# RMSNorm and matmul on one core: one 3 MB store cut by partitions into 22 DMAs, 16 of them issued by GpSimd

## The chip, the cores and the metric

The kernel runs on one core of a Trainium2 chip. The core has five engines that run their own instruction streams: TensorE (PE) for matrix products, VectorE (DVE), ScalarE (ACT), GpSimd (POOL) and SyncE (SP). Data moves between the main memory and the core's on-chip memory by DMA: an instruction on one of the engines' queues (SP, ACT or POOL) starts a transfer, and 16 DMA engines carry it out. The metric is the device time of one execution in microseconds, median of several runs. The time before is 208.85 us (208.76 to 209.47 in 3 runs).

## The reference

```python
rms = np.sqrt(np.mean(x ** 2, axis=-1, keepdims=True) + eps)
x_norm = x / rms * gamma
return np.matmul(x_norm, weight).astype(np.float32)
```

x is 16 x 1024 x 512, the weight is 512 x 768, all float32. Flattened, there are 16,384 rows of x: 33.6 MB in, 50.3 MB of results out, and a weight of 1.6 MB.

## The kernel before

**Tiles.** The rows are cut into 128 tiles of 128 rows, one row of a tile on each of the 128 partitions. `rows` (L121) fixes which rows form a tile: inside a group of 16 (or 32) tiles, one partition holds 16 (or 32) neighbouring rows of x, so that a partition's share of eight tiles is one contiguous piece of main memory, 16,384 bytes of x or 24,576 bytes of the result.

**One tile's way.** Loads bring 8 tiles at a time into `xt` (two halves of 16 tiles). POOL casts them to bf16 (`cast`, L188). PE turns them, two bf16 values as one 32-bit word (`transpose_word`, L230), and DVE copies the turned words out (`evac`, L239). Of every 16 tiles the last four go another way: POOL casts them into `xq` (`cast_quad`, L260) and DVE turns them in 32 x 32 blocks (`move`, L271). PE multiplies a tile with the weight (`matmuls`, L300) into one of three accumulators. ACT squares the tile and sums along the row (L196), takes a root (L201), DVE inverts it (L203); the row's factor is applied when the accumulator is read out into `ot`: by ACT for even tiles (L279), by DVE for odd ones (L281). Gamma is folded into the weight at the start.

**The result's way out.** `ot` has three buffers of 8 tiles, taken in turn: tiles 16 to 23 lie in the third one, and tiles 40 to 47 use it next. `store` (L293) issues a DMA on SP's queue when the last tile of a stretch has been written. A stretch has 8 tiles, except at the start (1, 1, 2, 4) and at the end (4, 4, then 4, 2, 2). The kernel has 22 stores, 13 of them of 3,072 KB. Loads from tile 32 on are issued on ACT's queue (L177).

**Order.** Nothing here is scheduled by a tool: the main loop over pairs of tiles (j = 1 to 63; pair j is tiles 2j and 2j + 1) hands each operation to an `Order` object with the cells that it reads and writes. `Order.emit` then writes the streams in just that order, and puts a wait ahead of an operation for each earlier one that its engine doesn't yet know to be done (L93). A DMA counts as a process of its own: each is waited for by itself, on its own semaphore value. So the first operation that overwrites a buffer waits for every DMA that read it. Semaphores are used again for a later DMA once the issuing engine knows the earlier one to be done.

POOL's own stream holds the casts of x, two at a time or more ahead of their use, and no DMA.

## Time and profile before

| | |
|---|---|
| median of 3 runs | 208.85 us |
| the profiled execution's own time | 209.07 us |
| its span, first to last instruction | 207.1 us |
| granted TensorE clock, mean | 0.993 |
| moved by DMA | 85.62 MB, 413 GB/s over the span |
| busy: PE / DVE / ACT / POOL | 194.7 / 149.5 / 144.3 / 60.0 us |

The span of the profiled execution lies 2.0 us under its own time. A line of the profile names an engine, a line of the kernel and the tile written and read (`ot<-ps,rstd` writes `ot` from the accumulators). "SPq", "ACTq" and "POOLq" stand for the queue's own work: issuing a DMA, or waiting on a semaphore. In the list of DMA queues, q1 holds what SP issues and q10 what ACT issues; the "instruction" queues fetch the program itself. Times inside the profile count from the span's start.

### The profile page before, as it was taken

Reading aid. Unit: us, or ns where it says so; the run is one execution under the profiler, and the core shown is the slowest. Engines: PE = TensorE matmul, PEld = TensorE weight load, DVE = VectorE, ACT = ScalarE, POOL = GpSimd, SP = SyncE. Lnnn points to the kernel's source line nnn. Section 1 sums busy time; section 2 is a strip of 40 time slices with the busy share of each in tenths; the row PEclk is TensorE's granted clock in tenths of the full one; section 3 lists DMA queues with packets and bytes.
Section 4 is the critical chain, followed back from the end, with each engine's and each line's share of the span. In section 5 each row is a group of like instructions: output and inputs, shape, how many; then the busy total and the mean of one; then the engine's idle time right before and its main releaser. Section 6 shows DMA issues by size and latency. Waiting matters only on the chain.

```text
span 207.1 us, 2794 instructions
## 1 busy us (share of the span) xinstructions
PE 194.7 (94%) x1236; PEld 72.7 (35%) x717; DVE 149.5 (72%) x255; ACT 144.3 (70%) x343; POOL 60.0 (29%) x34
## 2 busy tenths in 40 slices
PE   7789999999999999999999999999999989999940
PEld 1233434343334334433344333443343324333310
DVE  0446556999579975999579975999569964999530
ACT  4598898777777687777777687676949758683310
POOL 2156752157006340065105170060604224000000
PEclk9999999999999999999999999999999999999997
DMA  6999999999999999999999999999999999999992
GB/s 222 402 434 453 370 419 420 426 461 407 437 429 423 449 419 440 419 434 429 432 449 411 430 434 423 445 423 437 413 424 445 427 440 435 423 437 394 394 412 120
DMA packets 6064, 85.62 MB, mean 413 GB/s; under 512 B 674, under 2 KB 676, under 8 KB 1828
## 3 DMA queue, kind: packets, MB, share of 16 engines
q1 hardware_dynamic: 4320, 60.30, 68.9%
q10 hardware_dynamic: 1732, 25.17, 28.5%
q8 instruction: 7, 0.11, 0.2%
q14 instruction: 5, 0.04, 0.0%
HBM read 35.13 MB, written 50.33 MB: 413 GB/s over the span
## 4 chain that ended last, share of the span: by engine, by line
PE 71%; DMA 17%; DVE 5%; SPq 1%; issue 1%; POOL 1%; ACT 0%; ACTq 0%
PE ps L300 63%; DMA out_dram<-ot 12%; PE ps L230 8%; DMA xt<-in_x_dram 5%; DVE ot L281 2%; DVE xTq L271 2%; DVE xT L239 1%; POOL xb L188 1%; SPq L345 0%; ACT ot L279 0%; SPq L177 0%; DVE rstd L203 0%; SPq L477 0%; ACTq L93 0%; SPq L436 0%
## 5 line engine op out<-in xcount | busy, mean ns | idle before, releaser
L300 PE MATMUL ps<-w_bf,xT 128*128 128x512 bf16 (+1 forms) x800 | 147.9, 326 | 2.1 <-DVE w_bf L281 1.1
L279 ACT ACTIVATE ot<-ps,rstd 128x768 f32<-128x768 f32 x64 | 57.6, 899 | 48.5 <-PE ps L300 37.3
L196 ACT ACTIVATE jk<-xt 128x512 bf16<-128x512 f32 x128 | 78.7, 619 | 1.9 <-DMA xt<-in_x_dram 1.9
L188 POOL CAST xb<-xt 128x2048 bf16<-128x2048 f32 (+3 forms) x21 | 46.4, 2218 | 112.4 <-PE ps L230 69.0
L281 DVE TENSOR_SCALAR ot<-ps,rstd 128x768 f32<-128x768 f32 x64 | 64.8, 1013 | 9.5 <-PE ps L300 8.1
L296 PEld LDWEIGHTS <-xT 128*128 128x128 bf16 x400 | 39.3, 98 | 60.7 <-issue 52.8
L230 PE MATMUL ps<-ident_f,xb 128*128 128x128 f32 x200 | 54.4, 276 | 0.9 <-POOL xb L188 0.9
L239 DVE COPY xT<-ps 128x1024 bf16<-128x1024 bf16 (+1 forms) x53 | 34.5, 654 | 24.2 <-PE ps L230 22.5
L271 DVE STREAM_TRANSPOSE xTq<-xq 32x256 f32<-32x256 f32 x112 | 48.8, 435 | 3.4
L230 PEld LDWEIGHTS ps<-ident_f,xb 128*128 128x128 f32 x200 | 28.3, 143 | 46.6 <-issue 43.3
L300 PE MATMUL ps<-w_bf,xTq 128*128 128x512 bf16 x224 | 42.8, 326 | 0.0
L196 ACT ACTIVATION_READ_ACCUMULATOR jk<-xt 128x1 f32 x128 | 24.4, 190 | 0.0
L296 PEld LDWEIGHTS <-xTq 128*128 128x128 bf16 x112 | 11.0, 98 | 14.5 <-issue 14.5
L260 POOL CAST xq<-xt 128x2048 bf16<-128x2048 f32 x7 | 13.3, 1893 | 0.0
L203 DVE RECIPROCAL rstd<-rms 128x8 f32<-128x8 f32 (+3 forms) x20 | 3.9, 193 | 8.1 <-ACT rms L201 7.9
L201 ACT ACTIVATE rms<-ssq,eps_sb 128x8 f32<-128x8 f32 (+3 forms) x20 | 6.0, 300 | 0.6
L300 PE MATMUL ps<-warm 128*128 128x512 bf16 x10 | 4.5, 588 | 1.4 <-DVE eps_sb L354 1.4
L279 ACT ACTIVATE w_bf<-w_f,g_sb 128x768 bf16<-128x768 f32 x2 | 1.9, 935 | 1.8 <-DMA w_f<-in_weight_dram 1.8
L377 DVE COPY g_sb<-ps 128x4 f32<-128x4 f32 x1 | 0.2, 163 | 3.2 <-PE ps L371 3.2
L341 ACT ACT_TABLE_LOAD x1 | 1.3, 1283 | 1.5 <-SPq L436 1.5
L281 DVE TENSOR_SCALAR w_bf<-w_f,g_sb 128x512 bf16<-128x512 f32 (+2 forms) x3 | 1.4, 482 | 1.2 <-DMA w_f<-in_weight_dram 1.2
L371 PEld LDWEIGHTS ps<-ident_f,g_row 2*128 2x128 f32 x2 | 0.3, 200 | 2.6 <-issue 2.6
(10 smaller groups left out, 2.0 us busy)
## 6 DMA issues: line engine op xcount, KB each, us to landing
out_dram<-ot SPq DMA_DIRECT2D x13, 3072.0 KB, 22.7
xt<-in_x_dram ACTq DMA_DIRECT2D x12, 2048.0 KB, 18.8
xt<-in_x_dram SPq DMA_DIRECT2D x3, 2048.0 KB, 18.2
out_dram<-ot SPq DMA_DIRECT2D x4, 1536.0 KB, 10.9
out_dram<-ot SPq DMA_DIRECT2D x3, 768.0 KB, 6.8
w_f<-in_weight_dram SPq DMA_DIRECT2D x2, 768.0 KB, 5.9
xt<-in_x_dram SPq DMA_DIRECT2D x2, 512.0 KB, 5.4
xt<-in_x_dram SPq DMA_DIRECT2D x1, 1024.0 KB, 9.5
```

The source lines that it names most:

```text
L188: run(POOL, lambda: POOL.tensor_copy(out=xb[s][:, i % 8:i % 8 + n, :], in_=src), of, cells("xb", s, i % 8, n))
L196: run(ACT, lambda: ACT.activation(out=jk[j], in_=src[:, 0, :], func=AF.Square, accum_out=ssq[:, i:i + 1]), of, [("jk", j), ("ssq", i)])
L201: run(ACT, lambda: ACT.activation(out=rms[:, s], in_=ssq[:, s], func=AF.Sqrt, scale=1.0 / D, bias=eps_sb), [("ssq", t) for t in range(i, i ...
L203: run(DVE, lambda: DVE.reciprocal(out=rstd[:, s], in_=rms[:, s]), [("rms", i)], [("rstd", t) for t in range(i, i + n)])
L230: run(PE, lambda: PE.transpose(out=tp[b][:, t, h, :], in_=words[:, lo:lo + P], identity=ident_f), cells("xb", s, j % 4 * 2 + t) + ["ident" ...
L239: run(DVE, lambda: DVE.tensor_copy(out=dst[:, t:t + n, :], in_=src[:, t:t + n, :]), [("tp", b)], cells("xT", j % 4, t, n))
L260: run(POOL, lambda: POOL.tensor_copy(out=xq[s], in_=src), of, [("xq", s)])
L271: run(DVE, lambda: DVE.transpose(out=dst, in_=src), [("xq", s)], [("xTq", s)])
L279: run(ACT, lambda: ACT.mul(out=dst, in_=src, mul=r), reads, writes)
L281: run(DVE, lambda: DVE.tensor_single_scalar(out=dst, in_=src, scalar=r, op=mybir.AluOpType.mult), reads, writes)
L296: run(PE, lambda: PE.ldweights(lhsT), [cell])
L300: run(PE, lambda: PE.add_instruction(mybir.InstMatmult(name=nc.get_next_instruction_name(), engine=mybir.EngineType.PE, ins=[PE.lower_ap(r ...
```

## The change

Only the store of tiles 16 to 23 is changed (`first == XG`, with XG = 16). Before, it is one DMA on SP's queue: 128 partitions, 24,576 bytes of each. After, it is 22 DMAs. Each takes partitions that lie four apart. For p = 0, 1, 2, SP stores partitions p, p + 4, ... p + 24 (seven of them), and the row of partition p + 28 is stored in two halves of 8 x 1,536 bytes, one by SP and one by POOL. For p = 3, 32, 33, 34 and 35, POOL stores the eight partitions p, p + 4, ... p + 28. For all eight p, POOL stores the eight partitions from p + 64 on. SP's six DMAs are issued where the one store was. POOL's sixteen are kept in a list, and put into the order after the next `cast_quad`, that is in the pass j = 15 of the main loop, behind the cast of tiles 44 to 47. A DMA issued by POOL gets a semaphore that no DMA has used before it.

```diff
             if proc is None:
                 free = [k for k, d in enumerate(slots) if known[at].get(("transfer", d), 0)]
-                if free:
+                if free and engine is not nc.gpsimd:
                     slots[free[0]] = n
...
+    later = []
+
+    def spread(dst, src, held):
+
+        def part(engine, p, n, cols=slice(0, O)):
+            at = slice(p, p + 4 * n - 3, 4)
+            move = lambda: order.transfer(engine, lambda: engine.dma_start(out=dst[at, :, cols], in_=src[at, :, cols]), reads=held)
+            later.append(move) if engine is POOL else move()
+
+        for p in (0, 1, 2, 3, 32, 33, 34, 35):
+            if p < 3:
+                part(SP, p, 7)
+                part(SP, p + 28, 1, slice(O // 2, O))
+                part(POOL, p + 28, 1, slice(0, O // 2))
+            else:
+                part(POOL, p, 8)
+            part(POOL, p + 64, 8)
+
     def store(i):
...
             src = ot[s][:, first % OG:first % OG + n, :]
+            if first == XG:
+                spread(rows(out, first, n), src, cells("ot", s, first % OG, n))
+                return
             order.transfer(SP, lambda: SP.dma_start(out=rows(out, first, n), in_=src), reads=cells("ot", s, first % OG, n))
...
             cast_quad((2 * j + 2 + XG - 4) // 4)
+            while later:
+                later.pop(0)()
```

## The prediction

> **What bounds the kernel now.** I read the row of DMA load on the page first, then the busy times by stage, then the waits from the middle on, then the last microseconds, and last the places that the change touches.

> ```profile
> DMA  6999999999999999999999999999999999999992
> ```

> The row holds the mean load of the 16 DMA engines in 40 slices: full from the second slice to the last but one. By stage (columns: stretch, its length, busy us of PE, PEld, DVE, ACT, POOL with counts, granted clock, DMA share, GB/s):

> ```profile
> 50.00:74.00 24.00, 24.00 (x157) 9.08 (x90) 19.62 (x34) 18.05 (x44) 6.90 (x4) 1.00 1.01 432
> 74.00:130.00 56.00, 56.00 (x366) 21.30 (x211) 43.76 (x73) 41.81 (x100) 15.58 (x7) 1.00 1.01 430
> 130.00:168.00 38.00, 37.98 (x247) 14.30 (x142) 32.22 (x56) 26.04 (x63) 10.93 (x4) 1.00 1.00 429
> 168.00:200.00 32.00, 30.28 (x194) 10.76 (x108) 23.49 (x37) 19.63 (x42) 3.73 (x2) 1.00 0.98 418
> 200.00:203.50 3.50, 0.00 (x0) 0.00 (x0) 0.10 (x1) 0.00 (x0) 0.00 (x0) 1.00 0.94 384
> 203.50:205.70 2.20, 0.00 (x0) 0.00 (x0) 0.00 (x0) 0.00 (x0) 0.00 (x0) 0.67 0.06 25
> ```

> Up to 130 PE and the DMA engines are both full. The last line is the odd one: for 2.2 us all five engines are idle and the DMA share is 0.06, one engine in sixteen. The DMA queues in that stretch (packets, MB, share) and the two rows around it:

> ```profile
> q1 hardware_dynamic: 11, 0.06, 6.1%
> ...
> 200.40 0.33 SPq L293 DMA_DIRECT2D out_dram<-ot  x1
> ...
> SPq L477 <- DMA out_dram<-ot: 5.4, 1, 5.4
> ```

> The last store is issued at 200.40. By the trace's packets fifteen engines write their last byte of it by 203.45. One goes on alone with packets of 6,144 bytes, 231 ns apart, until 205.68, and SP waits for it. So 2.2 us of the span belong to a single DMA engine. It is late before the end too. The store issued at 142.43 lands, by the trace's sixteen completions, in three bunches: seven engines at 164.7 to 165.5, eight at 166.3 to 166.6, and one at 167.9. That last one ends a wait of ACT, because tile 104 needs the buffer:

> ```profile
> 142.43 25.50 DMA out_dram<-ot
> ...
> 168.01 0.91 ACT ot L279
> ...
> ACT ot L279 <- DMA out_dram<-ot: 9.5, 4, 3.1
> ```

> ACT has four such waits, 9.5 us in all, all after 128. PE hardly feels them. Its stretches without transposes (36 matmuls) start at 46.69, 70.11, 93.53 and 116.95 in the chain, 23.42 apart for 16 tiles. Three periods after the last the next should start at 187.21, and it starts at 188.32: PE loses 1.1 us to the end.

> The places that the change touches (POOL's rows; one of SP's; ACT's and DVE's first writes into the buffer when it comes round again; a wait instruction; a store's median landing time):

> ```profile
> 48.60 1.89 POOL L260 CAST xq<-xt 128x2048 bf16<-128x2048 f32 x1
> 64.11 3.60 POOL L188 CAST xb<-xt 128x4096 bf16<-128x4096 f32 x1 [13.62 <-PE ps L230]
> ...
> 48.74 0.33 SPq L293 DMA_DIRECT2D out_dram<-ot  x1
> ...
> 71.78 0.90 ACT L279 ACTIVATE ot<-ps,rstd 128x768 f32<-128x768 f32 x1 [0.70 <-PE ps L300]
> 73.58 1.02 DVE L281 TENSOR_SCALAR ot<-ps,rstd 128x768 f32<-128x768 f32 x1
> ...
> L93 ACTq EVENT_SEMAPHORE  x46: 17/17/17, 4.3 to 187.2; - x46
> ...
> out_dram<-ot SPq DMA_DIRECT2D x13, 3072.0 KB, 22.7
> ```

> The store of tiles 16 to 23 is issued at 48.74 and lands at 69.5 by its completions. Tile 40 overwrites the buffer at 71.78.

> **The gain: three rows less on one DMA engine.** A 3,072 KB store is 128 packets of 24,576 bytes, eight an engine, 0.91 us each. SP's three DMAs of seven partitions leave out the eighth of their pattern, partitions 28, 29 and 30. If a row's partition fixes its engine, one engine loses three rows, 2.73 us, and gets back 6 pieces of 1,536 bytes, at 26.6 GB/s 0.35 us: 2.38 us less. Seven others gain 0.35 us each. If that engine is the late one, it ends at 203.3 instead of 205.68, and the others set the end at 203.45 to 203.8. They have idle time to take it from: a share of 0.98 over 168 to 200 is 0.6 us an engine. The end moves by 1.9 to 2.2 us; I take 2.0. The bytes are the same, so no more is to be had than that lag: the fifteen others are full.

> That the engine relieved is the late one no row says. What speaks for it is the shape of the landings, seven, eight and one, the split that the change makes between SP's seven partitions, POOL's eight from p + 64 on, and the one left over. I give it three in four.

> The waits of ACT on the late engine get shorter by its lag (1.3 us in the bunches above). They are worth at most PE's 1.1 us, and as the other DMA engines are full behind them, I count 0.

> **SP.** One issue of 0.33 us becomes six, 2.0 us, and SP then sits until its next store at 59.65: 0. The SP queue has 21.5 rows of this store instead of 128, so the next store finds a shorter queue.

> **POOL.** Sixteen DMAs follow the cast that ends at 50.49; tile 23 has been written by then. The next cast starts at 64.11, and its product is first turned in the pass j = 22, from about 77.2. So POOL has 13.6 us empty and about 9 us more before PE feels it (3.60 us of cast from 73.6). No DMA is issued by POOL in this profile, so its price p is open. The lower end is SP's issue, 0.33 us; the upper is POOL's cast of 128x2048, 1.89 us. I take 1.04, its cast of 128x1024, the middle one of its own rows: 16.6 us, to 67.1, the cast 3.0 us late, cost 0.

> [...]

> **When the pieces land.** Before tile 40 all 22 must have landed. A piece must start (the last store's first fifteen engines need 3.0 us from issue to their last byte, 1.85 of it data), wait for a packet of each other queue (0.91 and 0.61) and move 0.91: 3 us. At p = 1.04 the last lands at 50.5 + 16.6 + 3 = 70.1. At p = 0.33 the engines set the pace: between 50 and 72, q1 and q10 both have work, and their packet counts are alike:

> ```profile
> q1 hardware_dynamic: 258, 5.55, 58.9%
> q10 hardware_dynamic: 268, 3.87, 41.2%
> ```

> So queues take turns by packets. With a third one, eight rows need 8 x (0.91 + 0.91 + 0.61) = 19.4 us, 50.5 to about 71. Both are ahead of 71.78, and SP's own pieces stand behind only the store of 36.2, which lands at 57.4. Loads pay for it: up to 8 packets of 0.91 us, 7.3 us, on the load issued at 53.12. Its first user that can't wait is ACT's square of tile 56 at about 83, 12 us after it landed: 0.

> **Waits.** ACT at tile 40 and DVE at tile 41 wait for 22 DMAs instead of one. A wait lasts 17 ns and the next instruction follows 0.06 us after it begins: 21 x 0.06 = 1.3 us on each. They stand behind the wait for PE, so they start when the product is done. Behind them are queued the read-out and then ACT's squares, DVE's copies for PE. In this stretch a tile takes PE 1.3 us, and tile 43 needs tile 40's accumulator at about 74.3: ACT's read-out, which may start 1.6 us later than 71.78, is just covered, DVE's is some 0.3 us over. PE's 1.1 us of later waiting hide that; without them it costs 0.3 us.

> **Sum.** -2.0 us against the profiled execution's own 209.07 gives 207.1; against the median, which is 0.2 us lower, 208.85 - 2.0 = 206.9. For the likeliest case alone I give 206.3 to 207.7 (another 0.6 us from the waits at one end, 0.8 us of uncovered waits or SP pieces at the other). Less than 0.5% (1.04 us) can't be told from no change in this kernel.

> **Rivals.**
> *The late engine isn't the one relieved.* For it: the profile names no engine. Against it: the seven, eight and one. Then the lag stays, a few engines get 0.35 us more, and the time is 208.8 to 209.2.
> *POOL's eights lie the other way round.* If the engines that carry POOL's rows from p + 64 on are the ones with SP's seven, these get 3 + 8 rows instead of 8, three rows or 2.73 us more, end at 203.45 + 2.73 - 0.6 = 205.6, and no lag is saved: 208.8 to 209.4. Nothing in the profile tells which eight a POOL DMA gets.
> *POOL is too slow, and tile 40 waits.* The wait on the store that now costs ACT nothing at 71.78 becomes the bound. With 1.3 us of waits behind the landing, PE stalls once 50.5 + 16p + 3 is past 72.1, at p = 1.16. PE's 1.1 us cover it up to 1.23, the 2.0 us gained are gone at 1.35, and it is slower by 0.5% from 1.42 on. At 1.89 the last piece lands at 83.7, 11.6 us late: 208.85 + 11.6 - 1.1 - 2.0 = 217.3. For it: POOL's 128x2048 cast, 1.89 us, is past that point, and the margin above my 1.04 is small. Against it: POOL's rows that move little data (0.10 to 0.29 us) come nowhere near 1.4.

> [...]

> **How the numbers follow.** The likeliest case, 206.9, gets 0.52. The wrong engine gets 0.17 and the eights the other way 0.07, both within 0.5%. POOL too slow gets 0.24: 0.01 of it still faster, 0.02 within, 0.21 slower. That makes 0.53, 0.26 and 0.21. The range runs from 206.2, just under the likeliest case, to 211.0, which takes in both middle rivals and POOL up to p = 1.49; the 0.15 beyond it is POOL slower still, up to the 217.3 of its upper row.

> **What would show it.** Right: in the last store's landing all sixteen engines end within half a microsecond, and the stretch of 0.06 DMA share is gone; the chain ends in a DMA of about 3.5 us after its issue; POOL's cast of tiles 48 to 55 starts by 68; ACT's first write after 71 isn't preceded by a wait on a DMA. Wrong: the same lone engine at the end (first rival), several engines late at the end (second), or ACT and PE idle near 72 to 85, with POOL's last DMA issue after 70 (third). The prediction fails most easily by p, of which no row speaks.

## The result and the profile after

The changed kernel takes 232.30 us (median of 4 runs, 231.44 to 233.45) against 208.84 us before in the same comparison: a ratio of 1.112, with a 95% interval of 1.107 to 1.117. The forecast was 206.9 us, and the range ended at 211.0. The profiled execution took 232.22 us, with a span of 230.4 us. Of two kernels in the experiments (one DMA on GpSimd, sixteen partitions each on GpSimd) some executions took clearly longer than the rest; their times are given, but left out of the comparisons.

The first view is again the page's slices of the span: the granted TensorE clock and the load of the DMA engines, in tenths, 5.8 us a slice.

```profile
PEclk9999999999999655559999999999999999999996
DMA  6999999999999974236899999999999999869787
```

Before, the DMA row was full throughout. Now it has a hole from the 15th slice to the 20th, some 81 to 115 us, and the clock drops at its beginning. The table by stage shows the hole (columns: stretch, its length, busy us of PE, PEld, DVE, ACT and POOL with counts, granted clock, DMA share, GB/s):

```profile
68.00:74.00 6.00, 5.73 (x36) 1.88 (x19) 4.73 (x9) 2.12 (x5) 3.73 (x2) 1.00 1.01 383
74.00:84.00 10.00, 0.00 (x0) 0.00 (x0) 0.00 (x0) 0.00 (x0) 0.00 (x0) 0.63 0.96 397
84.00:97.00 13.00, 0.00 (x0) 0.00 (x0) 0.00 (x0) 0.00 (x0) 0.00 (x0) 0.50 0.43 185
97.00:101.00 4.00, 3.04 (x10) 0.68 (x5) 1.74 (x3) 3.99 (x10) 0.00 (x0) 0.50 0.00 0
101.00:105.00 4.00, 3.95 (x18) 1.43 (x11) 0.85 (x2) 1.74 (x5) 0.00 (x0) 0.64 0.74 254
```

From 74 to 97 no engine does anything. The second line still has the DMA engines full. In the third they are idle more than half of the time (0.43), although everything waits for a DMA. That is the line to remember: the transfer that all wait for keeps fewer than half of the DMA engines busy. In the fourth line the DMA engines have nothing at all, because the loads are issued on ACT's queue, and ACT has just come out of its wait: its next load goes out at 101.18.

What they wait for is in the waits (engine, line, releaser: us in total, times, longest) and in the chain of work from 45 to 100 (start, length, what):

```profile
ACT ot L279 <- DMA out_dram<-ot: 26.5, 1, 26.5
DVE ot L281 <- DMA out_dram<-ot: 24.0, 1, 24.0
PE ps L321 <- ACT ot L279: 24.2, 1, 24.2
```

```profile
49.94 7.71 POOL out_dram L294 x15
57.65 39.29 DMA out_dram<-ot
96.94 0.03 ACTq L93
96.97 0.05 issue
97.01 0.91 ACT ot L279
```

ACT's write of tile 40 stands behind the cut store, as it did before. Then the store landed at 69.5, ahead of its need at 71.78. Now its last piece lands at 96.9 and the write starts at 97.01. So 97.01 - 71.78 = 25.2 us are lost in one place. From that write to the end of the span it was 207.1 - 71.78 = 135.3 us before and is 230.4 - 97.01 = 133.4 us now: 1.9 us come back. The sum, +23.3, is the difference of the two spans.

The 1.9 us are nearly the lag of the lone engine at the end. SP's last wait is now

```profile
SPq L500 <- DMA out_dram<-ot: 3.0, 1, 3.0
```

where it was 5.4 us, and the sixteen completions of the last store lie within 0.2 us. That isn't the relief that the change was predicted to give. Every DMA engine had run dry at 101 us, and yet one was late again after that: of the store issued at 133.16, fifteen completions come by 146.6 and the last at 149.5. The lag went later, where the DMA engines had idle time (their share is 0.68 from 200 to 212). In the first experiment below, which was to load all engines alike, the last store's completions also lie within 0.2 us (219.5 to 219.7).

**Why the pieces land so late.** The two rows of POOL's queue on the timeline show that its issues aren't the cause:

```profile
49.88 8.29 POOL L294 DMA_DIRECT2D out_dram<-ot  x16
63.55 3.60 POOL L188 CAST xb<-xt 128x4096 bf16<-128x4096 f32 x1 [5.39 <-PE ps L230]
```

Sixteen issues take 8.3 us, 0.52 us each, and are over at 58.2. POOL then waits 5.4 us for PE before its next cast. The pieces themselves are slow, which their completions show. Each DMA of POOL gives sixteen, as many as there are DMA engines, though none has more than eight rows. For the later DMAs of eight partitions the trace has (us from the span's start):

```
DMA of POOL       eight early ones   eight late ones
p = 3 + 64        60.1 to  63.3      69.3 ... 74.6
p = 32            61.4 to  63.5      73.4 ... 78.6
p = 32 + 64       61.5 to  63.6      77.5 ... 82.8
p = 33            61.7 to  63.8      80.6 ... 85.4
p = 33 + 64       61.9 to  64.0      84.5 ... 88.0
p = 34            62.0 to  64.2      87.3 ... 90.7
p = 34 + 64       62.2 to  64.4      90.0 ... 93.5
p = 35            62.4 to  64.5      92.7 ... 95.5
p = 35 + 64       62.6 to  64.7      93.6 ... 96.9
```

By these times eight engines have nothing to move. The other eight have one row, and each DMA's are a step later than those of the DMA ahead of it. If successive DMAs used different engines, their late completions would run side by side; they run one after the other. So all 13 DMAs lie on one set of eight engines. In each row the first of the late ones is ahead of the second by 0.7 to 2.8 us (80.6 against 83.4 for p = 33): one engine of the set has less to do than the others, as it would if SP's three DMAs of seven partitions used the same set and left one engine out. SP's next store, issued at 59.09, says so too: eight of its completions come at 71.0 to 73.0, one at 80.0 and seven at 83.0 to 86.0. Seven engines therefore carry 3 + 13 = 16 rows of this store, where each had eight; eight engines carry none.

The second thing is the pace. In the last column the steps are 4.0 to 4.2 us at first (74.6 to 82.8) and 2.6 to 2.7 later (82.8 to 93.5), for a row that takes 0.91 us to move. On the first of the late engines the last step is 0.9 us (92.7 to 93.6), the row alone. The DMA queues in two stretches (packets, MB, share of 16 engines), first 72 to 82, with loads (q10), stores of SP (q1) and POOL's pieces (q0), then 84 to 96, where the loads have ended:

```profile
q1 hardware_dynamic: 93, 2.21, 52.8%
q10 hardware_dynamic: 93, 1.39, 36.1%
q0 software_dynamic: 40, 0.49, 11.9%
```

```profile
q1 hardware_dynamic: 73, 1.52, 29.6%
q0 software_dynamic: 76, 0.88, 17.4%
```

In the second, q1 and q0 have the same number of packets, 73 and 76, but not the same bytes: 0.88 MB are 36 rows of 24,576 bytes, and the other 40 of q0's 76 packets are writes of 4 bytes, the signals to the semaphores. The changed kernel has 1,088 packets of 4 bytes where the kernel before has 675. A DMA that brings one row to an engine brings it two packets, the row and the signal, and if each must wait for its own turn, a row costs two rounds of the other queues: 0.91 + 2 x (0.91 + 0.61) = 3.95 us with q1 and q10 busy, 0.91 + 2 x 0.91 = 2.73 with q1 alone. These are the two longer steps measured. The trace's packets show the signal's own turn. Five of them, one after the other (start, length, bytes, queue):

```
85.814  0.912  24,576  q0
86.722  0.912  24,576  q1
87.631  0.009       4  q0
87.636  0.912  24,576  q1
88.545  0.912  24,576  q0
```

The trace doesn't number the DMA engines, so that these five share one is read from their times. It is no accident of one place: of the 20 rows of q0 that end from 84.5 to 92, 19 have a signal of q0 0.88 to 0.93 us behind their end, and of the 23 signals 22 have a row of q0 as long behind them. From 72 to 82, with the loads, the same gaps are 1.51 to 1.58 us, behind 17 of 20 rows and 18 of 20 signals.

One set for all 13 DMAs is what the completions above show. By what rule they are dealt out so, and which engines the set has, no run here shows.

### The profile page after: what moved, and what is told of

Its sections match the earlier page's. It is cut to its first block, busy times and chain, and to the rows that moved or that the text cites. A ratio compares the mean times of both kernels' runs of the same rounds, so it can differ in the third digit from the quotient of the medians.

```text
span 230.4 us, 2811 instructions
## 1 busy us (share of the span) xinstructions
PE 195.7 (85%) x1212; PEld 72.9 (32%) x717; DVE 149.2 (65%) x255; ACT 144.6 (63%) x343; POOL 68.2 (30%) x50
## 3 DMA queue, kind: packets, MB, share of 16 engines
q10 hardware_dynamic: 1732, 25.17, 26.6%
## 4 chain that ended last, share of the span: by engine, by line
PE 69%; DMA 21%; POOL 5%; issue 1%; SPq 1%; DVE 0%; ACT 0%; ACTq 0%
PE ps L321 61%; DMA out_dram<-ot 17%; PE ps L230 8%; DMA xt<-in_x_dram 4%; POOL out_dram L294 3%; POOL xb L188 1%; POOL xq L260 1%; DVE ot L281 0%; ACT ot L279 0%; SPq L366 0%; SPq L177 0%; SPq L500 0%; ACTq L93 0%; SPq L459 0%
## 5 line engine op out<-in xcount | busy, mean ns | idle before, releaser
L321 PE MATMUL ps<-w_bf,xT 128*128 128x256 bf16 (+1 forms) x783 | 146.2, 327 | 26.2 <-ACT ot L279 24.2
L279 ACT ACTIVATE ot<-ps,rstd 128x768 f32<-128x768 f32 x64 | 57.6, 899 | 74.3 <-PE ps L321 46.1
L281 DVE TENSOR_SCALAR ot<-ps,rstd 128x768 f32<-128x768 f32 x64 | 64.8, 1013 | 34.1 <-DMA out_dram<-ot 24.0
L188 POOL CAST xb<-xt 128x2048 bf16<-128x2048 f32 (+3 forms) x21 | 46.4, 2218 | 125.6 <-PE ps L230 107.3
L230 PE MATMUL ps<-ident_f,xb 128*128 128x128 f32 x200 | 54.4, 275 | 0.9 <-POOL xb L188 0.9
L321 PE MATMUL ps<-w_bf,xTq 128*128 128x256 bf16 (+1 forms) x217 | 43.4, 333 | 0.4
L230 PEld LDWEIGHTS ps<-ident_f,xb 128*128 128x128 f32 x200 | 28.3, 142 | 47.3 <-issue 44.0
L317 PEld LDWEIGHTS <-xTq 128*128 128x128 bf16 x112 | 11.2, 100 | 15.3 <-issue 15.3
L260 POOL CAST xq<-xt 128x2048 bf16<-128x2048 f32 x7 | 13.3, 1894 | 0.0
L294 POOL DMA_DIRECT2D out_dram<-ot x16 | 8.3, 526 | 0.0
L279 ACT ACTIVATE w_bf<-w_f,g_sb 128x768 bf16<-128x768 f32 x2 | 1.9, 936 | 1.4 <-DMA w_f<-in_weight_dram 1.4
L281 DVE TENSOR_SCALAR w_bf<-w_f,g_sb 128x512 bf16<-128x512 f32 (+2 forms) x3 | 1.4, 481 | 0.8 <-DMA w_f<-in_weight_dram 0.8
## 6 DMA issues: line engine op xcount, KB each, us to landing
out_dram<-ot SPq DMA_DIRECT2D x12, 3072.0 KB, 16.3
```

Of the source, the lines that this page charges most:

```text
L188: run(POOL, lambda: POOL.tensor_copy(out=xb[s][:, i % 8:i % 8 + n, :], in_=src), of, cells("xb", s, i % 8, n))
L230: run(PE, lambda: PE.transpose(out=tp[b][:, t, h, :], in_=words[:, lo:lo + P], identity=ident_f), cells("xb", s, j % 4 * 2 + t) + ["ident" ...
L260: run(POOL, lambda: POOL.tensor_copy(out=xq[s], in_=src), of, [("xq", s)])
L279: run(ACT, lambda: ACT.mul(out=dst, in_=src, mul=r), reads, writes)
L281: run(DVE, lambda: DVE.tensor_single_scalar(out=dst, in_=src, scalar=r, op=mybir.AluOpType.mult), reads, writes)
L294: move = lambda: order.transfer(engine, lambda: engine.dma_start(out=dst[at, :, cols], in_=src[at, :, cols]), reads=held)
```

## The experiments

All of these kernels compute the whole result. Only the store of tiles 16 to 23 (once, the last two stores) is issued in another way. Each ran beside the kernel before on the same chip, which took 208.8 to 208.95 us.

### Sixteen partitions a piece, all on GpSimd

If uneven engines are the cause, pieces of sixteen partitions, by the author's estimate one row for each engine, must take it away.

```diff
-            at = slice(p, p + 4 * n - 3, 4)
+            at = slice(p, p + 8 * n - 7, 8)
...
-        for p in (0, 1, 2, 3, 32, 33, 34, 35):
-            if p < 3:
...
-            part(POOL, p + 64, 8)
+        for p in range(8):
+            part(POOL, p, 16)
```

> The store of tiles 16 to 23 as eight DMAs of 16 partitions each (p, p+8, ... p+120), all issued by GpSimd at the place where the changed kernel issues its sixteen; nothing of it on SP. Theory A (uneven load: every eight-partition DMA runs on the same eight DMA engines, 13 to 16 rows there instead of 8, and none on the other eight): with 16 partitions a DMA the load is even, the store lands by about 72, ACT waits under 3 us for it at tile 40, and the time is 208 to 210.5 us. Rival B (GpSimd's queue is slow in itself, whatever the engines): more bytes than before go by that queue, the store lands near 96 or later, and the time is 230 us or more. Rival C (the many waits and pieces cost it): eight waits instead of 22, so about a third of the 23 us loss, 214 to 218 us.

Measured: 223.0 us (222.81, 223.00 and 224.13; a fourth execution took 227.12), ratio 1.070, interval 1.065 to 1.074. None of the three ranges expected holds it. The wait at tile 40 ends at 87.5 instead of 97.0 (timeline of this kernel):

```profile
87.48 0.90 ACT L279 ACTIVATE ot<-ps,rstd 128x768 f32<-128x768 f32 x1 [15.95 <-DMA out_dram<-ot]
```

Of the 23.4 us lost, 9.3 are won back and 14.1 stay. If every engine holds eight rows, as that estimate has it, unevenness can't explain the rest. Two things stand out in the trace: between 45 and 100 us 80 of 481 packets of 24,576 bytes took more than 1.2 us, up to 3.2 (before, 1 of 574 did), and again each row has a signal of its own (q0's 256 packets with 3.15 MB are 128 rows and 128 signals). The next runs separate these.

### The same 22 pieces, all on SP

```diff
-            move = lambda: order.transfer(engine, lambda: engine.dma_start(out=dst[at, :, cols], in_=src[at, :, cols]), reads=held)
+            move = lambda: order.transfer(SP, lambda: SP.dma_start(out=dst[at, :, cols], in_=src[at, :, cols]), reads=held)
...
```

> The same 22 pieces at the same places of the order, but all issued on SP's queue; nothing is issued by GpSimd. Theory A (eight-partition DMAs share one set of eight DMA engines, on any queue): these engines still carry 16 rows of the store instead of 8, now in line on SP's queue; tile 40 waits for it for about 10 us or more, the stores after it on SP are late too, and the time is 213 to 230 us. Rival B (GpSimd's queue is slow): no such wait, 208 to 210.5 us, plus at most some us if SP's issues at 1 to 2 us each (20 to 30 us in all) are late.

Measured: 217.16 us (one run), 8.3 us over the kernel before. From the waits and the timeline of this kernel:

```profile
ACT ot L279 <- DMA out_dram<-ot: 11.7, 1, 11.7
```

```profile
82.25 0.90 ACT L279 ACTIVATE ot<-ps,rstd 128x768 f32<-128x768 f32 x1 [11.73 <-DMA out_dram<-ot]
```

The unevenness is there without GpSimd: SP's own eight-partition pieces leave the next store's completions split into eight at 79.8 to 82.1 and eight at 87.2 to 89.4. So a narrow set of engines isn't a peculiarity of GpSimd's queue. SP's pieces go to eight engines too. SP needed 17.0 us to issue the 22 pieces, but the last of them was out by 65.2, 17 us ahead of its landing, so issuing isn't what made it late. What the move to GpSimd's queue adds is 232.3 - 217.2 = 15.1 us. On SP's queue a piece stands behind other pieces of the same queue and takes turns with the loads alone: 0.91 + 2 x 0.61 = 2.13 us a row by the two-turn rule. Measured were 2.1 to 2.2 for the rows that land from 71.5 to 76, and 0.7 to 1.0 for the last five, when the load had ended on these engines.

### Half of the pieces over all engines

```diff
-            part(POOL, p + 64, 8)
+            if p < 4:
+                part(POOL, p + 64, 16)
```

> The changed kernel with one part altered: partitions 64 to 127 go as four DMAs of 16 partitions (64, 68, ... 124 and so on) instead of eight of eight partitions. The same bytes are issued by GpSimd. Theory A: the loaded eight DMA engines get 9 rows from GpSimd instead of 13 (12 with SP's), the other eight get 4. Nine rows at the 3 us or so that each took land near 80, tile 40 waits 7 to 13 us, and the time is 214 to 222 us, about half of the loss. Rival B (GpSimd's queue is slow by bytes): 230 us as with the change.

Measured: 221.0 us (one run), the wait at tile 40 ends at 87.3. Halving the excess rows (four instead of eight) saves 11.3 us of the 23.4, as the uneven-engines theory expects. But pieces of sixteen partitions have a cost of their own, as the first run showed, so this run isn't a clean measure of the dose. The next one is.

### Half of the unevenness, on SP alone

Tiles 16 to 19 as one DMA of all partitions, tiles 20 to 23 as sixteen DMAs of eight partitions, so that eight engines have an excess of four rows instead of eight.

```diff
+            if first == XG:
+                dst, held = rows(out, first, n), cells("ot", s, first % OG, n)
+                order.transfer(SP, lambda: SP.dma_start(out=dst[:, 0:4, :], in_=src[:, 0:4, :]), reads=held)
+                for p in (0, 1, 2, 3, 32, 33, 34, 35):
+                    for at in (slice(p, p + 29, 4), slice(p + 64, p + 93, 4)):
+                        order.transfer(SP, lambda at=at: SP.dma_start(out=dst[at, 4:8, :], in_=src[at, 4:8, :]), reads=held)
+                return
```

> The kernel before, with the store of tiles 16 to 23 on SP as one DMA of four tiles and 128 partitions and sixteen DMAs of eight partitions and four tiles. Theory A (every eight-partition DMA uses the same eight DMA engines): these carry 12 rows instead of 8, the others 4: half the excess of the run with all 22 pieces on SP. That run lost 8.3 us with 16 rows; the excess work is 3.6 us here against 7.3 us, so 2.5 to 6 us are lost, 211.3 to 215 us, and eight of the sixteen completions of the next store come some us after the other eight. Rival (the loss comes from the number of pieces on SP, 17 here and 22 there): 214 to 217 us.

Measured: 212.98 us (one run).

```profile
77.88 0.90 ACT L279 ACTIVATE ot<-ps,rstd 128x768 f32<-128x768 f32 x1 [7.26 <-DMA out_dram<-ot]
```

On SP, an excess of 0, 4 and 8 rows' worth of bytes on eight engines costs 0, 4.0 and 8.3 us, about 1.0 us a row, near the 0.91 us that it takes to move. A cost per piece would have stayed near that of the 22 pieces, since there are still 17 (214 to 217 us was expected for it). The store after it again has eight completions at 76.0 to 81.0 and eight at 84.0 to 85.2. The uneven engines are thus shown as a cause, by the completions and by the size of the loss, though each of the two sizes is from one run.

### The sixteen-partition pieces, on SP

```diff
-            at = slice(p, p + 4 * n - 3, 4)
-            move = lambda: order.transfer(engine, lambda: engine.dma_start(out=dst[at, :, cols], in_=src[at, :, cols]), reads=held)
+            at = slice(p, p + 8 * n - 7, 8)
+            move = lambda: order.transfer(SP, lambda: SP.dma_start(out=dst[at, :, cols], in_=src[at, :, cols]), reads=held)
...
-        for p in (0, 1, 2, 3, 32, 33, 34, 35):
...
+        for p in range(8):
+            part(POOL, p, 16)
```

> The eight DMAs of 16 partitions (p, p+8, ... p+120) of the first experiment, all issued on SP's queue at the same place; GpSimd issues no DMA. The load is even and the queue is the ordinary one. [...] Rival B (only GpSimd's queue made the first experiment slow): packets stay at 0.91 us, the store lands by 72, and the time is 208.3 to 210 us.

Measured: 211.81 us (one run), 2.9 us over the kernel before.

```profile
76.43 0.90 ACT L279 ACTIVATE ot<-ps,rstd 128x768 f32<-128x768 f32 x1 [5.68 <-DMA out_dram<-ot]
```

The pattern of every eighth partition is slow in itself: 50 of 547 packets took over 1.2 us, up to 3.0. The landing is late on two engines most of all: fourteen have completed the last piece by 72.8, the two others at 75.3 and 76.4. Why such packets are slow is not shown. The remaining 223.0 - 211.8 = 11.2 us of the first run come from moving the same pieces to GpSimd's queue.

### The whole store as one DMA on GpSimd

Is a third queue costly by itself, without any cut?

```diff
...
+        later.append(lambda: order.transfer(POOL, lambda: POOL.dma_start(out=dst, in_=src), reads=held))
```

> The whole store of tiles 16 to 23 as one DMA of 128 partitions issued by GpSimd, at the place where the changed kernel issues its sixteen. Two theories after the first three runs. Theory T (turns by packet, and a DMA's semaphore write takes a turn like a packet): a DMA that gives each DMA engine one row has two turns a row, one with eight rows has nine turns for eight. A row then needs 0.91 us of its own and one packet each of SP's and ACT's queue, 2.43 us; eight rows land 19 to 21 us after 51, near 71, tile 40 waits under 2 us, and the time is 208.3 to 210.3 us. Rival B (GpSimd's queue is served slowly whatever it holds, one row in 3 to 4 us as in the changed kernel): 8 rows take 24 to 32 us, landing at 76 to 84, tile 40 waits 4 to 12 us, and the time is 211 to 220 us.

> The one DMA of 128 partitions on GpSimd once more, for its time: the first time it gave 211.3 us once, and 214.9 to 215.4 three times. Theory T (an even DMA on GpSimd costs little): the store lands at 71 to 75 and the time of the undisturbed runs is 211 to 211.6 us, 2.5 us over the kernel before, because one DMA engine falls behind by 3 us on this store. Rival: 214.9 us and more in every run, so that the single 211.3 was the exception.

Measured in both together, nine executions: 210.5, 211.3, 212.6 and 212.9 us, and five of 214.7 to 219.9. By the first four the third queue by itself costs 1.5 to 3.9 us (the second run's ratio is 1.011, interval 1.003 to 1.020, or 2.3 us), and not 15; why the other five took longer is not known. None of the nine lies above 219.9, where the sixteen pieces took 232.3. The time is over the range of the theory of turns (208.3 to 210.3) and mostly inside the rival's (211 to 220), and none of the second run's executions lies in the 211 to 211.6 expected for it, so it doesn't decide between them; the landings do. The profile is of an execution of 215.3 us. The queues from 58 to 70:

```profile
q0 software_dynamic: 97, 2.14, 41.7%
q10 hardware_dynamic: 101, 1.57, 30.6%
q1 hardware_dynamic: 61, 1.43, 28.4%
```

Here q0's packets are whole rows (2.14 MB are 87 of them, so some ten of the 97 packets are signals), and nearly as many as q10's. Its store keeps its share, and fifteen engines land it at 68.6 to 71.3, in time, where the rival had 76 to 84. One engine lands at 74.3, and that one makes tile 40 wait.

### Two DMAs on GpSimd, with rows half as long

If a queue's turn is a packet, halving the packet halves the share of the queue. If turns are by bytes, nothing changes.

```diff
...
+        for t in (slice(0, 4), slice(4, 8)):
+            later.append(lambda t=t: order.transfer(POOL, lambda: POOL.dma_start(out=dst[:, t, :], in_=src[:, t, :]), reads=held))
```

> The same store as two DMAs of 128 partitions and four tiles each, issued by GpSimd at the same place: rows of 12,288 bytes, sixteen packets for a DMA engine instead of eight, the same bytes. Theory T (turns by packet, whatever its size): 16 turns of 0.46 + 0.91 + 0.61 = 1.98 us and two for the semaphores, 32 to 34 us, land at 83 to 86; tile 40 waits 11 to 14 us and the time is 216 to 222 us. Rival B (a queue's rate in bytes is what counts): as with one DMA, within 1.5 us of that run.

Measured: 219.97 us (one run); the store lands at 85.3. The queues from 58 to 70, and DVE's first write into the buffer:

```profile
q10 hardware_dynamic: 140, 2.05, 40.0%
q1 hardware_dynamic: 65, 1.57, 30.6%
q0 software_dynamic: 140, 1.52, 30.0%
```

```profile
85.42 1.02 DVE L281 TENSOR_SCALAR ot<-ps,rstd 128x768 f32<-128x768 f32 x1 [12.34 <-DMA out_dram<-ot]
```

q10 and q0 have 140 packets each, and q0's share of the time falls from 41.7% to 30.0%. With packets of half the size, in only two DMAs of all 128 partitions, the store lands 11 us later than with whole rows (85.3 against 74.3). By the equal counts, turns go by packets here, with rows of 24,576 bytes (97 against 101) as with rows of 12,288 (140 against 140). That a signal of 4 bytes takes such a turn too has no run of its own. It is shown by the packets of the changed kernel above, and the three steps of 3.95, 2.73 and 2.13 us fit it.

### Which engine is late at the end?

The last two stores of the kernel before, cut so that single engines would be left out of some pieces:

```diff
+            cuts = {NT - 4: (112, 119, 128), NT - 2: (120, 128)}.get(first)
+            if cuts:
+                dst, held = rows(out, first, n), cells("ot", s, first % OG, n)
+                for lo, hi in zip((0,) + cuts, cuts):
+                    order.transfer(SP, lambda lo=lo, hi=hi: SP.dma_start(out=dst[lo:hi], in_=src[lo:hi]), reads=held)
+                return
```

> The kernel before, with its last two stores (2 tiles each, rows of 6,144 bytes) cut so that the number of packets tells the DMA engines apart: the last but one into 112, 7 and 9 partitions, the last into 120 and 8, all on SP. [...]

Measured: 210.67 us (one run). The run doesn't answer: the time is 1.85 us over the kernel before, the cut stores' completions are spread over about 1 us, and in this execution two engines were late, where the kernel before had shown one (of the store issued at 191.56, two completions come at 198.2 and 198.5 and the others by 196.7).

### One engine relieved, by another cut

The store of tiles 16 to 23 on SP, its second half as 120 and 8 partitions.

```diff
+            if first == XG:
+                dst, held = rows(out, first, n), cells("ot", s, first % OG, n)
+                for lo, hi, t in ((0, 128, slice(0, 4)), (0, 120, slice(4, 8)), (120, 128, slice(4, 8))):
+                    order.transfer(SP, lambda lo=lo, hi=hi, t=t: SP.dma_start(out=dst[lo:hi, t, :], in_=src[lo:hi, t, :]), reads=held)
+                return
```

> The kernel before, with the store of tiles 16 to 23 on SP in three DMAs: four tiles of 128 partitions, the other four tiles of 120 partitions (fifteen engines with eight half rows each) and of the last 8 partitions (one half row more for each of eight engines). [...]

Measured: 212.09 us (211.48 to 212.59), ratio 1.015, interval 1.013 to 1.016. That is 3.3 us over the kernel before. One engine, as the one left out would, becomes the first to land, 2.2 and 3.0 us ahead of the next in the load and the store that follow (77.6 against 80.6 in the store), so a relief can be built. Whether it was the late one the run doesn't show: of the last store thirteen completions now come by 208.7 and three at 209.1 to 209.7. And the cut costs more than a relief could bring: 31 packets of 12,288 bytes took over 0.7 us, up to 4.3, where 0.46 is usual.

## Why the prediction was wrong

**The step that failed first** stands under "The gain: three rows less on one DMA engine": one engine loses three rows, "seven others gain 0.35 us each". No run shows that partitions 28, 29 and 30 lie on one engine, nor the 0.35 us. It also takes POOL's DMAs of eight partitions to fall on two sets of engines, eight rows on each engine as before. The completions show one set for all of them, the set that SP's pieces use. Seven engines carried eight rows more, 8 x 0.91 = 7.3 us by the price of a row, and eight carried eight rows less. Forecast for the seven was +0.35 us. On SP's queue alone that excess cost 8.3 us.

**The second** is the pace under "When the pieces land". A row was to cost one round, 2.43 us, and eight rows 19.4 us, to about 71. It cost 3.9 to 4.2 us while both other queues had work and 2.6 to 2.7 after, and there were 13 of them on each engine. That turns go by packets was read rightly from 258 and 268 packets before. That a piece of one row on its engine brings its signal as a second packet was missed. Where a DMA has eight rows on each engine and one signal behind them, as the one DMA on GpSimd (q0's 144 packets are 128 rows and 16 signals), the forecast of about 71 was right for fifteen engines (68.6 to 71.3). The doubled turns and the third queue's own cost fit the 15.1 us between the pieces on SP and on GpSimd; the split between them isn't measured.

**The rivals.** "POOL's eights lie the other way round" had the right kind of cause, which engines a POOL DMA gets, at a chance of 0.07. It was priced at three rows and 208.8 to 209.4 us, since it too let the eights from p and from p + 64 on fall on different sets; the possibility that all share one set was never asked. "POOL is too slow, and tile 40 waits" named the place and the symptom, ACT and PE idle from 72 on, but not the cause: POOL's last issue ended at 58.2, not after 70. Its upper bound of 217.3 was a bound on the issue price alone, so the range didn't reach.

**What held.** POOL's price p was 0.52 us, within 0.33 to 1.89 and half of the 1.04 taken; its next cast started at 63.55, not late. SP's six issues took 8.7 us, 0.9 to 1.9 each, and not the 2.0 forecast, but cost nothing: SP's next store went out at 59.09. Loads had the slack claimed for them: ACT's waits for loads are 1.8 us in all, where they were 1.9.

**Waits.** The 21 further waits were put at 1.3 us on ACT and DVE. From the last landing to ACT's write there is 0.1 us. The waits are passed one after another as the pieces land, so only the last one's cost shows; they do not queue up behind a store that is late.

**Sums.** Two small ones are off and change nothing. SP keeps 22.5 rows of the store, not 21.5. The three terms for a piece to land (1.15 us to start, 1.52 to wait, 0.91 to move) make 3.6 us, not 3.

**The lone engine.** Its 2.2 us at the end did go, but where the DMA engines had idle time, after one of them had been 2.9 us late again at 149.5. That the change relieves the late engine was never tested: as eight- and seven-partition pieces use one set of eight engines, this cut loads that set instead of unloading one of its members. Which engine is late, and whether it is always the same, stays open: one execution had one, others had two or three.

**The sum as measured.** Uneven engines, on SP: +8.3. The same pieces moved to GpSimd's queue: +15.1. Together that is the whole difference, the 1.9 us won back at the end included. Both figures hang on one run of the pieces on SP. Of the 15.1 us, the one even DMA on GpSimd's queue accounts for some 2.3 by its faster executions. The two turns a row are the explanation that fits the rest.

## What to carry to other kernels

Before a transfer is cut by partitions, find out from the completions of one piece which DMA engines carry it: here all 13 of eight partitions went to the same eight, and the store had landed when these were done, at 96.9, 32 us after the last of the other eight completions (64.7). The queues took turns by packets here (97 against 101, and 140 against 140), so a piece that gave an engine one row used every second turn for its signal (2.6 to 4.2 us a row, where 2.43 was forecast), and the third queue's store fell behind when its rows were halved (landed at 85.3 instead of 74.3). Ask of every buffer that comes round again how many microseconds its store may be late; here it was 2.3, and nearly all lateness beyond that went into the time.
